# A block with dilated attention and a gated delta rule on one core: exponentials of the second half of heads taken as one wide block, and probabilities turned by a diagonal matrix of reciprocals

## The chip, the cores and the metric

The kernel runs on one core of one Trainium2 chip. The metric is the device time of one execution in microseconds (us), given as the median of several runs. Engines are named as in the profile: PE is TensorE's matmul, PEld its weight load, DVE is VectorE, ACT is ScalarE, POOL is GpSimd, SP is SyncE, which issues the DMAs.

## The reference

The reference computes one transformer block on 1024 tokens of width 1024 in float32. The input is normalised and modulated, and one projection makes queries, keys and values for 8 attention heads and for 8 delta-rule heads of width 64. Then:

```
# attention, per head and per branch (window, dilation)
s = where(valid, q k^T / 8 + bias, -1e30);  e = exp(s - max)
o_i, lse_i = e v / sum(e), max + log(sum(e));  o = sum_i softmax(lse)_i o_i

# gated delta rule, per head, in chunks of 64 tokens
q, k, v = silu(causal_conv(...));  q, k scaled by 1/|q|, 1/|k|
decay[c,e] = exp(gcum[c] - gcum[e])        for c >= e
a = tril(beta k k^T * decay, -1);  (u, w) = (I + a)^-1 (beta v, beta k exp(gcum))
qk = tril(q k^T * decay)
state scan over chunks:  v' = u - w S;  o = (q exp(g)) S + qk v';  S = S exp(g_last) + (k exp(g_last - g))^T v'
```

Both outputs are projected by `w_out`, added to the input, and a gated feed-forward layer with a last normalisation follows.

## The kernel before, in words

**The stages.** The three attention branches are merged into one masked softmax with a summed bias. Large products split each float32 operand into a high and a low part of type fp32r and add three products (lines 582-616, 1589-1599). After the input normalisation the delta rule is done in two halves of four heads, `delta(0)` and `delta(1)` (line 1207), then attention for 4 pairs of heads and 8 query blocks (`attend`, line 1369), the output projection, the feed-forward layer with a seven-product scheme on halves, and the end.

**What sets the order of the work.** A scheduler puts each engine's instructions in an order of its own: what is written first goes first, and what is written later is taken forward where the earlier work isn't ready and its buffers are free. `urgent()` gives a block precedence. `tc.issue_after(x)` puts instructions behind `x` on the same engine and adds no other wait. A generator, `others()` (line 1148), hands out the projections that the latency-bound stages are filled with: z of half 0, then k, q and v of the second half of the delta heads, then z of half 1 (`z1`), then the attention projections. Small products stand in `with turn(name)` (line 576): the table `FILL` (line 43) says how many us of that generator are written ahead of a name, and the small products go behind the last product so written. `"trq3_0False": 2.56` stands ahead of the last transposes of `delta_early`, `"kk1_0_0_q": 6.4` and `"trv2_0": 12.8` ahead of products of `delta(1)`. The results of the generator go through two PSUM banks (`gbank`, line 147, tag `g`, `bufs` 2).

**The z projection.** `proj_t` (line 602) makes 128x256 outputs, eight per half, of 24 products each. `z_evac` (line 630) empties the bank with a Silu on ACT (line 634), and POOL scales the result by a gain.

**The second half of the delta heads.** `delta_early` (line 1195), written at the end of `delta(0)`, loads four tiles of projections (k, k, q, q), does the causal convolution (`conv`, line 550: a scaled copy on ACT, three multiply-adds on DVE, a Silu on ACT), turns the tile on PE for the squared norms (`delta_turn`, line 729) and stores it in DRAM (`cv`). The tiles `cv0` to `cv3` have the tag `dt` of pool `pr`, which has two buffers. `delta(1)` loads them again, and `delta_prep` (line 754) makes the decay factors. `delta_rows` (line 704) broadcasts the rows of the summed gates `G` from DRAM to four 128x1024 tiles (one for each head, tag `lu`, five buffers), and POOL masks them (line 716). For half 1, ACT takes the logarithm of the squared norms (line 765) and, by an exponential of -0.5 of it, the factors `rk` (line 767). Then ACT makes 32 exponentials of 128x128 (line 771), whose per-partition bias carries both the factor of the key and minus the gate sum. The products of keys and queries (line 800) are multiplied by these tiles (line 806). Two more broadcast tiles, `eb`, also with the tag `dt`, are loaded and exponentiated (lines 830-839) and scale the queries. `delta_v` (line 845) convolves the values, `delta_inverse` (line 867) inverts the triangular matrices, and `delta_scan` (line 973) runs over the eight chunks.

**Attention.** `att_score` (line 1295) makes one head's 128 rows of scores (two fp32r products for each bank), a DVE instruction adds the bias and takes the row minimum (line 1312), ACT exponentiates and sums the rows (line 1317), DVE takes the reciprocal of the sum (line 1318), and POOL multiplies the row block `X` by it in place (line 1319). `att_turn` (line 1324) turns every 128x128 block of `X` on PE against the identity (line 1332), and ACT or DVE copies the banks out (lines 1335, 1337). `att_value` (line 1340) multiplies by the values (line 1353).

## Time and profile before

| what | us |
|---|---|
| runs | 1403.87, 1399.05, 1405.15; median 1403.87 |
| the profiled execution's own time | 1399.13 |
| its span, first to last instruction | 1397.3 |
| second half of delta heads: `delta_early` to the values' transposes | about 277 to 345 in the span |
| attention, with projections as fill | about 478 to 662 |
| output projection left over, second part, norm | about 662 to 750 |
| feed-forward layer | about 750 to 1397 |

Times in rows of the profile are us from the first instruction of the span, unless marked ns. A group row ends with its busy time and the mean ns of one instruction, and behind a second bar stand the idle time ahead of it and what ended most of that. A row of the view by source line or tile gives the shortest, median and longest duration in ns and the first and last start. A row of the timeline gives start, duration, engine and line, with a count where neighbours are merged. TensorE's fp32 products appear as more than one record each, so counts of records and of calls in the code can differ. "128*128" is the part of the array that is used.

### The profile page before, as it was taken

The page shows a single profiled execution, that of the slowest core. Times are in us where ns is not written, and L with a number is a line of the kernel's source. Part 1 is how long each engine was busy: PE and PEld are TensorE (multiplying, and loading weights), DVE is VectorE, ACT ScalarE, POOL GpSimd, SP SyncE. Part 2 cuts the span into 40 slices and gives each one's busy share as a digit, 9 for nine tenths or more (in the row PEclk, how much of TensorE's full clock was granted, in tenths as well). Part 3 has the DMA queues.
Part 4 walks back from the last instruction along what each step waited for, and adds up shares of the span by engine and source line. Part 5 has one row for each costly group of instructions (what it writes and reads, how often), then busy time and mean ns, then how long its engine had stood idle before and what let it go on. Part 6 is the DMA issues. An engine that isn't in the chain of part 4 may idle for free.

```text
span 1397.3 us, 24428 instructions
## 1 busy us (share of the span) xinstructions
PE 1343.9 (96%) x8984; PEld 1109.9 (79%) x8984; DVE 878.8 (63%) x1677; ACT 661.4 (47%) x1287; POOL 283.6 (20%) x267
## 2 busy tenths in 40 slices
PE   8999999998999899999999999999999999999998
PEld 5778877888888777778877788888888888888876
DVE  3688484656836433676238977667575776474497
ACT  4498424356234254775157633333333333444455
POOL 2346412443213244443262000000000000000000
PEclk9999999999999999999999999999999999999999
DMA  8666575486352455541584355455453665766585
GB/s 310 230 190 168 160 212 168 131 259 184 106 152 69 124 141 177 152 110 58 187 269 151 113 159 181 158 163 173 133 200 108 213 210 191 255 222 192 195 262 197
DMA packets 169872, 245.68 MB, mean 176 GB/s; under 512 B 32566, under 2 KB 73831, under 8 KB 169752
## 3 DMA queue, kind: packets, MB, share of 16 engines
q1 hardware_dynamic: 169752, 244.12, 55.3%
q8 instruction: 71, 1.16, 0.3%
q14 instruction: 49, 0.40, 0.1%
HBM read 181.30 MB, written 67.48 MB: 178 GB/s over the span
## 4 chain that ended last, share of the span: by engine, by line
PE 53%; DVE 5%; DMA 3%; issue 2%; ACT 2%; POOL 1%; SPq 0%; DVEq 0%; ACTq 0%; POOLq 0%
PE wua L1596 9%; PE wga L1596 8%; PE X L1796 6%; PE wuc L1596 4%; PE wgc L1596 4%; PE wo L590 4%; PE g_a L590 3%; PE wgb L1596 2%; PE Z L1796 2%; PE Y L1796 2%; PE wub L1596 2%; PE y L1353 2%; PE tr L1332 2%; PE S L1308 1%; PE S L1309 1%
## 5 line engine op out<-in xcount | busy, mean ns | idle before, releaser
L1586 DVE TENSOR_TENSOR wl_db<-wr_db,wh_db 128x512 fp32r<-128x512 f32 x77 | 52.9, 690 | 66.4 <-ACT wh_db L1585 66.4
L1585 ACT CAST wh_db<-wr_db 128x512 fp32r<-128x512 f32 x77 | 47.4, 620 | 85.7 <-PE X L1796 39.4
L1312 DVE CUSTOM_DVE_ANT_0 X<-S,ng 128x512 f32<-128x512 f32 (+3 forms) x64 | 36.9, 587 | 57.2 <-PE S L1309 43.7
L1319 POOL TENSOR_SCALAR X<-X,sc 128x128 f32<-128x128 f32 (+7 forms) x64 | 48.7, 764 | 76.3 <-DVE sc L1318 72.3
L1796 PE MATMUL X<-wl_db,wh_da 128*128 128x512 f32 x160 | 62.4, 390 | 0.3 <-DVE wl_db L1586 0.3
L1796 PE MATMUL X<-wh_db,wl_da 128*128 128x512 f32 x160 | 62.3, 389 | 0.0
L1796 PE MATMUL X<-wh_db,wh_da 128*128 128x512 f32 x160 | 62.3, 389 | 0.0
L1317 ACT ACTIVATE X<-X,sc 128x128 f32<-128x128 f32 (+7 forms) x64 | 49.5, 775 | 24.3 <-DVE sc L1312 22.7
L1586 DVE TENSOR_TENSOR wl_da<-wr_da,wh_da 128x512 fp32r<-128x512 f32 x77 | 52.8, 685 | 3.7 <-ACT wh_da L1585 3.6
L1585 ACT CAST wh_da<-wr_da 128x512 fp32r<-128x512 f32 x77 | 47.5, 616 | 15.0 <-DMA wr_da<-ao_d 8.1
L590 PE MATMUL g_a<-hh,wh_a 128*128 128x512 f32 x128 | 52.7, 412 | 0.0
L590 PE MATMUL wo<-yl,wh_wo 128*128 128x512 f32 x128 | 50.6, 396 | 1.9 <-DVE yl L1416 1.9
L590 PE MATMUL g_a<-hh,wl_a 128*128 128x512 f32 x128 | 51.7, 404 | 0.0
L590 PE MATMUL wo<-yh,wh_wo 128*128 128x512 f32 x128 | 51.6, 406 | 0.0
L590 PE MATMUL g_a<-hl,wh_a 128*128 128x512 f32 x128 | 51.4, 401 | 0.0
L590 PE MATMUL wo<-yh,wl_wo 128*128 128x512 f32 x128 | 51.1, 399 | 0.0
L1332 PE MATMUL tr<-ident,X 128*128 128x128 f32 x288 | 45.8, 278 | 5.1 <-POOL X L1319 2.4
L1585 ACT CAST wh_wg_s<-wg_s 128x512 fp32r<-128x512 f32 x33 | 20.5, 623 | 57.6 <-PE wuc L1596 24.4
L1332 PEld LDWEIGHTS tr<-ident,X 128*128 128x128 f32 x288 | 32.8, 140 | 17.0 <-POOL X L1319 6.2
L231 POOL TENSOR_TENSOR wl_wo<-wr_wo,wh_wo 128x512 fp32r<-128x512 f32 x24 | 32.2, 1344 | 59.1 <-ACT wh_wo L230 54.9
L1585 ACT CAST wh_wu_s<-wu_s 128x512 fp32r<-128x512 f32 x33 | 20.4, 621 | 43.8 <-PE wga L1596 17.2
L1585 ACT CAST wh_wg<-wr_wg 128x512 fp32r<-128x512 f32 x31 | 19.2, 622 | 46.3 <-PE wua L1596 18.9
(553 smaller groups left out, 4370.0 us busy)
## 6 DMA issues: line engine op xcount, KB each, us to landing
wm<-in_wada SPq DMA_DIRECT2D x44, 512.0 KB, 6.3
wr_da<-ao_d SPq DMA_DIRECT2D x77, 256.0 KB, 3.1
wr_wu<-in_wu SPq DMA_DIRECT2D x50, 256.0 KB, 2.7
wr_wg<-in_wg SPq DMA_DIRECT2D x48, 256.0 KB, 2.9
ao_d<-a SPq DMA_DIRECT2D x44, 256.0 KB, 2.4
wr_wd<-in_wdn SPq DMA_DIRECT2D x44, 256.0 KB, 3.0
wr_db<-wt_d SPq DMA_DIRECT2D x44, 256.0 KB, 2.7
ao_d<-as SPq DMA_DIRECT2D x33, 256.0 KB, 2.0
```

The costliest lines, as they stand in the source:

```text
L231: (eng or nc.gpsimd).tensor_tensor(out=lo[:, :n], in0=raw[:, :n], in1=hi[:, :n].bitcast(F32), op=ALU.subtract)
L590: last[0] = nc.tensor.matmul(ps, a[:, w0], b[k0 + k4][:, cs], start=(i == 0), stop=(i == n - 1))
L1308: nc.tensor.matmul(ps[:, 0 : c1 - c0], QS[:, qs], KS[:, c0:c1], start=True, stop=False)
L1312: nc.vector.tensor_tensor_reduce(out=X[:, c0:c1], in0=ps[:, 0 : c1 - c0], in1=ng[:, u + c0 : u + c1], scale=1.0, scalar=(3e38 if m is None ...
L1317: nc.scalar.activation(X[:, 0:nk], X[:, 0:nk], AF.Exp, scale=-1.0, bias=m, accum_out=sc[:, 2:3])
L1319: nc.gpsimd.tensor_scalar(out=X[:, 0:nk], in0=X[:, 0:nk], scalar1=sc[:, 3:4], scalar2=0.0, op0=ALU.mult, op1=ALU.add)
L1332: nc.tensor.transpose(ps[:, (kb - c0) * P : (kb - c0 + 1) * P], X[:, kb * P : kb * P + P], ident)
L1353: ins = nc.tensor.matmul(yps[64 * e : 64 * e + 64, (q % 4) * P : (q % 4 + 1) * P], va[:, kb, 64 * e : 64 * e + 64], ets[q % 2][e][:, kb, : ...
L1585: nc.scalar.copy(hi, src)
L1586: (eng or nc.vector).tensor_tensor(out=lo, in0=src, in1=hi.bitcast(F32), op=ALU.subtract)
L1596: nc.tensor.matmul(ps, a[:, w0], b, start=(first and k == 0 and n_ == 0), stop=(k == 3 and n_ == 2), skip_group_check=True,)
L1796: nc.tensor.matmul(bank[b], a[:, ts_], w, start=(first and n_ == 0), stop=(last and n_ == 2), skip_group_check=True,)
```

## The change

Three things are done.

1. In attention, POOL's multiplication of `X` is gone. DVE makes a diagonal matrix `dg` (the identity times the reciprocals, 128x128), and each block of `X` is turned by an ordinary fp32 product with `dg` in place of the transpose against the identity.
2. For the second half of the delta heads, the rows of `G` and the two `eb` tiles are loaded in `delta_early` behind the last convolution, DVE subtracts the gate sums from the four row tiles, and ACT exponentiates the six tiles whole, one behind the other, after the last convolution's Silu. The Silus written after that (those of the values' convolution and of `z_evac`) are put behind the last of these exponentials on ACT. The factor of the keys is multiplied in by DVE in `delta_prep`.
3. For that half the inverse root of the squared norms is a power on POOL, in place of a logarithm and an exponential on ACT.

The store of a convolved tile to `cv` is written ahead of its transposes. The tile `mhalf` is wider by 12 columns, and a spare tile is narrower by as many.

```diff
@@ conv, z_evac
+    behind = [None]
...
-        nc.scalar.activation(dst, dst, AF.Silu)
+        with tc.issue_after(behind[0].ins) if behind[0] else ExitStack():
+            return nc.scalar.activation(dst, dst, AF.Silu)
...
-            with urgent():
+            with urgent(), tc.issue_after(behind[0].ins) if behind[0] else ExitStack():
                 taken[0] = nc.scalar.activation(zt, ps[:, 0:256], AF.Silu)
@@ delta_rows, behind the mask
+            if g:
+                nc.vector.tensor_tensor(
+                    out=dt_, in0=dt_, op=ALU.subtract,
+                    in1=bc(Gc[:, 32 * g : 32 * g + 32].rearrange("p (n h) -> p n h", n=8)[:, :, hl_], P),
+                )
             dts.append(dt_)
         return dts
+
+    def delta_exps(last):
+
+        lts = delta_rows(1)
+        ebs = [delta_eb(1, q) for q in range(2)]
+        for t in (*lts, *ebs):
+            with tc.issue_after(last.ins):
+                last = nc.scalar.activation(t, t, AF.Exp)
+        behind[0] = last
+        return lts, ebs
+
+    def delta_eb(g, q):
+
+        eb = pr.tile([P, 8, P], F32, name=f"eb{2 * g + q}", tag="dt", bufs=2)
+        for e in range(2):
+            nc.sync.dma_start(
+                eb[64 * e : 64 * e + 64],
...
+            )
+        return eb
@@ delta_turn
+        if norms and kind == "k" and g:
+            v = norms["rk"][:, :, 2 * q : 2 * q + 2]
+            nc.gpsimd.tensor_scalar(out=v, in0=v, scalar1=EPS, scalar2=None, op0=ALU.add)
+            nc.gpsimd.tensor_tensor(
+                out=v, in0=v, in1=mhalf.rearrange("p (n e) -> p n e", e=2), op=ALU.pow,
+            )
@@ delta_prep
-        if g == 1:
-            nc.scalar.activation(lr, rk, AF.Ln, bias=eps1)
-        nc.vector.tensor_scalar(out=lr, in0=lr, scalar1=-0.5, scalar2=None, op0=ALU.mult)
-        nc.scalar.activation(rk, lr, AF.Exp)
-        nc.vector.tensor_tensor(out=lr, in0=lr, in1=g3(Gc), op=ALU.subtract)
-        for h in range(4):
-            for n in range(8):
-                nc.scalar.activation(lts[h][:, n], lts[h][:, n], AF.Exp, bias=lr[:, n, h : h + 1])
+        if g == 0:
...
+        else:
+            for h in range(4):
+                nc.vector.tensor_tensor(out=lts[h], in0=lts[h], in1=bc(rk[:, :, h], P), op=ALU.mult)
...
+            if ebs:
+                eb = ebs[q]
+            else:
+                eb = delta_eb(g, q)
+                nc.scalar.activation(eb, eb, AF.Exp)
@@ delta_early
-            conv((4 if kind == "k" else 0) + 2 + q, fetch(j, f"{kind}{2 + q}"), t)
+            last = conv((4 if kind == "k" else 0) + 2 + q, fetch(j, f"{kind}{2 + q}"), t)
+            nc.sync.dma_start(_.cv[j], t)
+            if j == 3:
+                made = delta_exps(last)
             delta_turn(1, kind, q, t, norms=norms[1])
-            nc.sync.dma_start(_.cv[j], t)
+        return made
@@ att_score, att_turn
-        nc.gpsimd.tensor_scalar(
-            out=X[:, 0:nk], in0=X[:, 0:nk], scalar1=sc[:, 3:4], scalar2=0.0, op0=ALU.mult, op1=ALU.add
-        )
-        return X
+        dg = pa.tile([P, P], F32, name=f"dg{h}_{qb}", tag="dg", bufs=4)
+        nc.vector.tensor_scalar(out=dg, in0=ident, scalar1=sc[:, 3:4], scalar2=None, op0=ALU.mult)
+        return X, dg
...
-                    nc.tensor.transpose(ps[:, (kb - c0) * P : (kb - c0 + 1) * P], X[:, kb * P : kb * P + P], ident)
+                    nc.tensor.matmul(
+                        ps[:, (kb - c0) * P : (kb - c0 + 1) * P], X[:, kb * P : kb * P + P], dg, start=True, stop=True,
+                    )
```

In the branch `g == 0` of `delta_prep`, the half 0 keeps the five statements that are removed above, without the logarithm, which it takes elsewhere.

More of the change, by code (lines that the diff above doesn't have):

```diff
@@ L1230, in delta @@
         delta_scan(g, st)
-        if g == 0:
-            delta_early()
-    delta(0)
-    delta(1)
+        return None if g else delta_early()
+    delta(1, delta(0))
     until(lambda: EARLY - 1 in done)
```

34 lines of the change are left out of this document (17 added, 17 removed).

## The prediction

> **What bounds the kernel now.** I read the page first (engines' shares), then the table by stretches, then the waits of PE in the two stages that the change touches.
>
> ```profile
> PE 1343.9 (96%) x8984; PEld 1109.9 (79%) x8984; DVE 878.8 (63%) x1677; ACT 661.4 (47%) x1287; POOL 283.6 (20%) x267
> ...
> 276.00:320.00 44.00, 40.43 (x395) 36.61 (x395) 22.88 (x44) 26.25 (x48) 19.94 (x20) 1.00 0.82 254
> 320.00:345.00 25.00, 20.94 (x214) 19.35 (x213) 17.39 (x22) 15.92 (x39) 9.29 (x7) 0.91 0.60 150
> 478.00:662.00 184.00, 174.66 (x1280) 140.09 (x1280) 96.94 (x314) 113.71 (x255) 78.16 (x82) 0.99 0.46 135
> 665.00:695.00 30.00, 30.00 (x140) 24.64 (x137) 8.21 (x11) 3.70 (x6) 6.43 (x5) 1.00 0.59 194
> ```
>
> The first row is the page's: PE is busy for 96% of the span. In the other rows the columns are stretch, length, busy us (instructions) of PE, PEld, DVE, ACT, POOL, then PE's granted clock. Attention (478 to 662) keeps PE busy for 174.7 of 184 us, and right behind it PE works without a gap on projections left over (665 to 695). So work added to PE in attention lengthens the kernel, except for what fits into 9.3 us of idle time. In the delta stage PE idles 3.6 us before 320 and 4.1 us after it, at a clock of 0.91. The waits of PE, from 478 to 662 and (last three rows) from 276 to 346:
>
> ```profile
> PE tr L1332 <- POOL X L1319: 2.4, 3, 1.0
> PE S L1308 <- DVE sc L1312: 2.0, 5, 1.1
> PE wo L590 <- DVE yl L1416: 1.9, 1, 1.9
> PE tr L1332 <- DVE et L1335: 1.9, 3, 0.9
> ```
>
> ```profile
> PE trv L857 <- ACT vd L557: 3.8, 1, 3.8
> PE yt L1065 <- DVE o L1055: 1.7, 3, 1.2
> PE kk_q L800 <- DMA qd<-cv_d: 0.9, 1, 0.9
> ```
>
> The POOL step that the change removes holds PE for 2.4 us in all. The exponentials that it widens hold PE only through the values' Silu behind them, 3.8 us.
>
> **Attention: what the product costs.** First the transposes of now and an ordinary fp32 product of the same shape (128x128 by 128x128) by source line, then two pieces of the timeline (start, length, records).
>
> ```profile
> L1332 PE MATMUL tr<-ident,X x288: 270/273/331, 487.8 to 660.8; 128*128 128x128 f32 x144
> ...
> L985 PE MATMUL st<-S,kd 128*128 128x128 f32 x56 | 11.8, 293 | 2.2 <-DVE S L1020 2.1
> ...
> 627.34 0.60 PE L1332 MATMUL tr<-ident,X 128*128 128x128 f32 x4
> ...
> 268.90 0.38 PE L985 MATMUL st<-S,kd 128*128 128x128 f32 x2
> ```
>
> The code calls the transpose 288 times (8 heads, 1 to 8 blocks for each of 8 query blocks), and there are 288 records: one each. Line 985 is called 28 times (7 chunks, 2 pairs, 2 halves) and has 56 records: two each. Records start (0.60 - 0.273) / 3 = 0.109 us apart in a row of transposes, and (0.38 - 0.273) = 0.107 us apart within one product. So a transpose holds PE for 0.109 us and a product for about twice that, and the change adds 288 x 0.109 = **31.4 us** to PE.
>
> The Trainium skill speaks against this edit in "Perfetto Trace Analysis", Transposes: a logical transpose should be a transpose and not a standard matmul. In "TensorE: Matmul & The Clock Gate", Terms, it calls the transpose mode 4x faster for FP32. By that factor the added work would be 288 x 3 x 0.109 = 94 us, an estimate; the records here show a factor of two, and I go by them.
>
> What is saved and added beside PE:
>
> ```profile
> L1319 POOL TENSOR_SCALAR X<-X,sc 128x128 f32<-128x128 f32 (+7 forms) x64 | 48.7, 764 | 76.3 <-DVE sc L1318 72.3
> ...
> L298 DVE TENSOR_TENSOR wbg<-wba,G 128x128 f32<-128x128 f32 x1 | 0.3, 293 | 0.0
> L1499 DVE TENSOR_TENSOR dg<-ident,r 128x512 f32<-128x512 f32 x2 | 1.4, 693 | 0.1
> ```
>
> POOL's 64 steps of 0.76 us go, and 64 diagonals come to DVE. The trace has no such instruction on one 128x128 tile with a per-partition scalar; the nearest is the 128x128 product of line 298 at 0.29 us, the other end is a quarter of the 128x512 diagonal of line 1499, 0.17. I take 0.29: 18.8 us on a DVE that is busy 97 of the stage's 184 us, hidden behind PE's own work; if that cover were gone, it would cost at most those 18.8, but POOL's 48.7 us lie at the same place in the chain and held PE for only 2.4. The chain to the transpose becomes 0.47 us shorter for each block of rows. With PE slower by a tenth in this stage, the other engines run ahead of it, so I take back the waits on POOL, on the scores and on the copies out: 2.4 + 2.0 + 1.9 = 6.3 us. Attention: 31.4 - 6.3 = **+25 us**. Bounds: all 9.3 us of PE's idle time absorbed, +22; nothing absorbed and the two DVE waits (3.9 us) doubled, +35.
>
> **The delta stage: what is saved on ACT.**
>
> ```profile
> L771 ACT ACTIVATE dt<-dt,lr 128x128 f32<-128x128 f32 x32 | 9.7, 397 | 0.0
> L557 ACT ACT_TABLE_LOAD x2 | 2.6, 1283 | 4.4 <-DVE vd L553 4.4
> L839 ACT ACTIVATE eb<-eb 128x1024 f32<-128x1024 f32 x2 | 2.1, 1054 | 0.4 <-issue 0.4
> ...
> L875 DVE TENSOR_TENSOR nt<-nt,bpr 128x1024 f32<-128x1024 f32 x2 | 2.4, 1221 | 14.7 <-POOL wl_qd L231 14.7
> L1053 POOL TENSOR_TENSOR of<-of,mhalf 128x4 f32<-128x4 f32 x16 | 16.3, 1016 | 20.3 <-DVE of L1050 20.2
> ```
>
> The 32 small exponentials (9.7 us busy) become four of 1.05, or 4.2 us. The logarithm and the small exponential go, and with them most of the changes between Silu's and the exponential's tables, of 1.28 us each. DVE gets eight 128x1024 operations by a broadcast factor, like line 875's 1.22 us: 9.8 us, four ahead of the exponentials and four ahead of the products with the keys. POOL's power is shown for 4 columns at 1.02 us; for 16 it is between 1.02 and 4.1, twice, and the key norms are done about 15 us before they are used, so I cost it at nothing; uncovered it would delay the products by up to 8 us. None of this is on PE's path except in front of the values' transposes: with the exponentials gone from behind 315 us, the values' convolution no longer has to follow them, and the wait of 3.8 us goes.
>
> **The delta stage: the wait that is added.** All Silus that are written after the wide exponentials go behind the last of them on ACT, whatever engine order the scheduler would choose. Which ones are these? Adding up the `FILL` entries in the order of the program, the generator stands in the last v projection when `delta_exps` is reached: the first product of `z1` is written by `"trq3_0False"`, just behind it. So all eight z evacuations of this half wait. In the trace they run early, as a filling of the scan and of the convolutions:
>
> ```profile
> L634 ACT ACTIVATE zt<-g_z x8: 361/381/384, 278.6 to 313.9; 128x256 f32<-128x256 f32 x8
> ...
> 282.45 0.28 PE L613 MATMUL g_z<-wh_z,hl 128*128 128x256 f32 x1
> 282.57 0.28 PE L613 MATMUL g_z<-wl_z,hh 128*128 128x256 f32 x1
> ```
>
> One z tile is 24 records 0.12 us apart, 2.9 us. Two fit into the two `g` banks, and the others can't start until the first bank is emptied. Six tiles, **17.3 us** of PE's work, are thus pushed behind the exponentials. When do these end?
>
> ```profile
> 302.53 2.59 DVE L553 SCALAR_TENSOR_TENSOR cv<-xp_q,cw,cv 128x1022 f32<-128x1022 f32 x2
> ...
> 306.54 1.06 ACT L557 ACTIVATE cv<-cv 128x1024 f32<-128x1024 f32 x1
> ...
> L1202 SPq DMA_DIRECT2D cv_d<-cv x2: 320/329/338, 303.1 to 307.6; - x2
> ...
> DMA to landing us min/median/max: 5.0/5.0/5.0
> ...
> L832 SPq DMA_DIRECT2D eb<-G_d x4: 627/634/685, 322.0 to 324.1; - x4
> ...
> DMA to landing us min/median/max: 5.1/5.1/5.1
> ```
>
> The last convolution ends on DVE at 305.1; its Silu no longer waits for table loads, so it ends at 306.2. The second `eb` tile needs a `dt` buffer, and both are in use: it gets that of `cv3`, which is free when its store has landed, 5.0 us later. Its load takes 5.1, the exponential 1.05, the table load back to Silu 1.28 and the first evacuation 0.38: about **319 us** in place of 278.6. The load sits in SP's queue meanwhile with what is issued after it, the loads of the stored tiles among them; those need the same store and lose little. From about 290, where the third z tile would run, until 319 PE has only transposes to do, and the products of keys and queries stand behind the fill of `"kk1_0_0_q"`, which needs the third z tile. So beside the 17.3 us about 3 us of work that PE did before 319 are late too (projections of va and the first of these products, whose place is seen in the wait at line 800): 20 us. After 319 PE has fill without end, and gets back the 3.8 us of the values' wait and some 1.5 of other short ones (its wait on DVE at line 1055 is 1.7). The delta stage: 20.3 - 5.3 = **+15 us**. Low bound: if the exponentials end so early that no z tile is late, only the 3.8 us stay, -4. High bound: if DVE's four subtractions stand ahead of the last convolution step, 4 x 1.22 = 4.9 us later, and 2 us of short waits come back less than I assume, +22.
>
> The clock: after the wait of 3.8 us the table's row 320 to 345 shows 0.91, which is 0.09 x 25 = 2.3 us lost. The new wait is longer, so I expect the same loss at about 320 and count no gain. The Trainium skill says in "TensorE: Matmul & The Clock Gate", HAM oscillation, that idle gaps over some 3.4 us bring the clock down; the row agrees, and by that page a gap of 20 us costs again one such stretch and the sum doesn't change.
>
> **The sum.** 25 + 15 = +40 us. Against the profiled execution's own time of 1399.13 that is 1439; this execution lies 4.7 us under the median of 1403.87, and from the median it is **1444 us**. Bounds: 22 - 4 = +18, or 1422; 35 + 22 = +57, or 1461. I widen the low side to 1417 for the rivals.
>
> **The rivals.**
> - *The z tiles are not held up*: the scheduler, or earlier loads, ends the exponentials near 300. For it: `G` rows are ready early, and only one `dt` buffer is critical. Against: the store and load of 10 us behind the last Silu. Then the delta stage gives -4 and the kernel takes 1403.9 + 25 - 4 = 1425. Chance 0.20.
> - *Faster: the chain of the row block, not PE, sets attention's pace.* Then the product's second record costs nothing, and each of 64 row blocks is 0.47 us shorter: -30, with the delta stage +15: 1389. It decides if PE's free time in the stage is over 31 us. For it: POOL is named ahead of the transposes. Against: PE idles 9.3 us, 2.4 of them behind POOL. Chance 0.05; the same with the chain half as long a limit, an end within 0.5%, has 0.02.
> - *The product takes four passes*, as the page's factor says: four records of 0.109 for each. Then 94 - 6 + 15 = +103, 1507. Against: two records for each call of line 985. Chance 0.03.
> - *The stall spreads*: ACT's order behind the exponentials also holds copies that PE needs, for another 15 us or more: over 1461. Chance 0.04.
>
> **How the numbers follow.** The forecast has 0.66. The range from 1417 to 1461 takes in the first rival and the forecast. A difference of 0.5%, 7 us, is about what can be told from no change here. Slower: 0.66 + 0.20 + 0.03 + 0.04 = 0.93; within: 0.02; faster: 0.05.
>
> **What would show it.** The products in place of the transposes: 576 records, 0.11 us apart, and PE's busy time up by some 31 us in attention, with its stretch about 25 us longer. All eight evacuations of the second z half behind the last of six exponentials of 1.05 us, at about 319 us; PE idle for some 20 us between 290 and 319, named as waiting for ACT; no wait of 3.8 us at the values' transposes. Wrong would be the forecast if the product had 288 records, if PE's idle time in attention fell by more than 10 us, or if z evacuations stood ahead of the exponentials.

## The result, and the profile after

| | before | after |
|---|---|---|
| median of runs, us | 1403.90 (1399.05 to 1405.15) | 1467.42 (1467.01 to 1473.01) |
| profiled execution / its span, us | 1399.13 / 1397.3 | 1467.23 / 1465.5 |

After against before is 1.0468 (95% interval 1.0433 to 1.0504), 63.5 us slower; the forecast was 40 us, 1444. The page after: engine totals, TensorE's clock in 40 slices of 36.6 us, and the group of the turns.

```profile
PE 1394.0 (95%) x9272; PEld 1158.4 (79%) x9272; DVE 903.7 (62%) x1747; ACT 654.3 (45%) x1253; POOL 241.5 (16%) x207
...
PEclk9998999967999999999999999999999999999999
...
L1366 PE MATMUL tr<-dg,X 128*128 128x128 f32 x576 | 77.2, 279 | 4.7 <-DVE et L1371 2.8
```

The 576 records are there. The clock row has a dip that the forecast does not account for: 6 and 7 in the ninth and tenth slice, 293 to 366 us, the second half of the delta heads. That place in the table by windows, columns as in the prediction, before and then after:

```profile
290.00:350.00 60.00, 52.93 (x510) 48.64 (x509) 38.30 (x49) 39.99 (x78) 23.42 (x19) 0.94 0.75 216
```

```profile
290.00:350.00 60.00, 37.83 (x361) 28.12 (x361) 30.35 (x46) 24.23 (x36) 19.71 (x14) 0.63 0.64 212
```

From 290 to 350 TensorE has 361 records instead of 510, at a clock of 0.63, and idles 22.2 us for 7.1. Where the time went is read from fixed points in the work (view by tile, first and last start): the transposes of the delta outputs (`yt`, the last ends the delta stage), the first turn of a stored tile, and the products with the values (the last ends attention). Before, then after:

```profile
L1065 PE MATMUL yt<-ident,o x32: 270/273/421, 255.9 to 475.5; 128*128 128x128 f32 x32
...
L738 PE MATMUL trk_0False<-ident,cv x8: 272/272/273, 292.3 to 294.0; 128*128 128x128 f32 x8
...
L1353 PE MATMUL y<-et,va x576: 272/273/476, 493.1 to 665.2; 128*64 128x128 f32 x192
```

```profile
L1099 PE MATMUL yt<-ident,o x32: 270/273/476, 264.7 to 509.8; 128*128 128x128 f32 x32
...
L769 PE MATMUL trk_0False<-ident,cv x8: 272/376/421, 313.8 to 315.9; 128*128 128x128 f32 x8
...
L1389 PE MATMUL y<-et,va x576: 272/273/323, 529.0 to 730.1; 128*64 128x128 f32 x192
```

The stored tiles are turned 21.5 us later (292.3 to 313.8), the delta stage ends 34.3 us later (475.5 to 509.8), attention 64.9 us later (665.2 to 730.1). So attention cost 30.6 us, near the forecast's 25, and the delta stage 34.3 where 15 was forecast. (These are differences of the two profiled executions, which lie 68.1 us apart, as that of before is 4.8 under its median.)

The same two parts as stretches of equal work, from 100 us to the last `yt`, and from there to the end of the output projection's last product `wo`. Before, then after:

```profile
100.00:475.50 375.50, 354.45 (x3483) 310.15 (x3484) 230.96 (x484) 166.49 (x366) 134.66 (x120) 0.98 0.53 154
475.50:751.30 275.80, 262.40 (x1734) 211.32 (x1735) 136.23 (x364) 152.84 (x323) 117.32 (x111) 0.99 0.51 155
```

```profile
100.00:509.80 409.80, 371.55 (x3488) 322.48 (x3487) 238.70 (x491) 157.86 (x334) 142.36 (x124) 0.92 0.47 142
509.80:821.90 312.10, 297.04 (x2022) 248.88 (x2022) 154.92 (x428) 155.52 (x323) 69.08 (x47) 0.99 0.45 137
```

In the first part nearly the same records (3483 and 3488) take 17.1 us more of busy time, at a clock of 0.92 for 0.98, and TensorE idles 17.2 us more. In the second part, which holds attention, there are 288 records more, 34.6 us more of busy time at the same clock, and almost the same idle time (15.1 us for 13.4). So attention is no different in kind from before: it has more work on a TensorE that was busy already.

Of the delta stage's loss a large part exists *before* the exponentials run: the convolution chain starts late. The timeline of SP's queue says by what, before and then after:

```profile
283.84 1.90 SPq L1120 DMA_DIRECT2D wm<-in_wada  x2
285.84 0.42 SPq L1045 DMA_DIRECT2D zl<-zg_d  x1
```

```profile
292.42 14.44 SPq L1154 DMA_DIRECT2D wm<-in_wada  x10
306.92 0.46 SPq L1079 DMA_DIRECT2D zl<-zg_d  x1
...
312.62 0.42 DVE L1089 TENSOR_TENSOR o<-o,zl 128x256 f32<-128x256 f32 x1 [5.31 <-DMA zl<-zg_d]
```

`wm` are weights of the modulation, whose products are one more filling of TensorE. Before, two of these loads stand ahead of the load of a gate tile `zl`, which the end of the first half's scan needs. After, ten do, and SP takes 14.4 us over them. The gate tile is loaded 21 us later, and VectorE waits for it (last row). TensorE's timeline of the same time, after:

```profile
295.44 1.08 PE L211 MATMUL mods<-wm,cc 128*32 128x128 f32 x32
298.36 0.99 PE L211 MATMUL mods<-wm,cc 128*32 128x128 f32 x16 [1.83 <-DMA wm<-in_wada]
...
312.29 1.08 PE L211 MATMUL mods<-wm,cc 128*32 128x128 f32 x16 [0.54 <-DMA wm<-in_wada]
313.30 0.69 PE L1099 MATMUL yt<-ident,o 128*128 128x128 f32 x2
313.79 1.06 PE L769 MATMUL trk_0False<-ident,cv 128*128 128x128 f32 x4
```

From 295 to 313 there is nothing but modulation, load by load; then the scan's output that needed the gate tile is turned, and behind it the first stored tile.

ScalarE behind the last convolution, after:

```profile
329.77 1.06 ACT L560 ACTIVATE cv<-cv 128x1024 f32<-128x1024 f32 x1 [2.04 <-DVE cv L555]
330.85 1.28 ACT L737 ACT_TABLE_LOAD   x1
332.14 3.90 ACT L737 ACTIVATE dt<-dt 128x1024 f32<-128x1024 f32 x4
...
341.80 1.06 ACT L737 ACTIVATE eb<-eb 128x1024 f32<-128x1024 f32 x1
342.88 1.28 ACT L637 ACT_TABLE_LOAD   x1
344.18 0.66 ACT L637 ACTIVATE zt<-g_z 128x256 f32<-128x256 f32 x2
```

The first evacuation of a z tile starts at 344.2, the last of the eight at 374.0; the forecast had the first end at about 319. The path from the last Silu to the start of the first has nearly the forecast's length: 344.18 - 330.83 = 13.4 us, against 12.4 (319 - 306.2, less the evacuation's own 0.38). The start of the path is wrong, by 24.6 us.

For the 22.2 us that TensorE idles from 290 to 350, the view by waits does not name the held evacuations. It names the loads of `wm` (5.9 us), the convolutions' Silus (5.7) and `nbp` (4.8), a factor that VectorE makes from the result of GpSimd's powers. The second power ends at 328.08, and `nbp` follows at 329.66. In e11 below, which has no power, the wait on `nbp` is 2.5 us. No run prices the power by itself.

A second, smaller delay is seen on VectorE at the first scan, before and then after:

```profile
248.53 0.94 DVE L1018 COPY S<-st 64x64 f32<-64x64 f32 x4 [4.33 <-PE st L1009]
```

```profile
253.48 2.28 DVE L724 TENSOR_TENSOR dt<-dt,Gc 128x1024 f32<-128x1024 f32 x1 [6.21 <-POOL dt L719]
255.77 0.95 DVE L1052 COPY S<-st 64x64 f32<-64x64 f32 x4
```

The first of the new subtractions stands ahead of the scan's first copy of the state. It waits 6.2 us for GpSimd's mask and takes 2.3, and the copy, 248.5 before, runs at 255.8.

### The profile page after: what moved, and what is told of

Same layout as the page of the kernel before. It is cut to its first block, busy times and chain, and to the rows that moved or that the text cites. A ratio compares the mean times of both kernels' runs of the same rounds, so it can differ in the third digit from the quotient of the medians.

```text
span 1465.5 us, 24871 instructions
## 1 busy us (share of the span) xinstructions
PE 1394.0 (95%) x9272; PEld 1158.4 (79%) x9272; DVE 903.7 (62%) x1747; ACT 654.3 (45%) x1253; POOL 241.5 (16%) x207
## 5 line engine op out<-in xcount | busy, mean ns | idle before, releaser
L1366 PE MATMUL tr<-dg,X 128*128 128x128 f32 x576 | 77.2, 279 | 4.7 <-DVE et L1371 2.8
L1366 PEld LDWEIGHTS tr<-dg,X 128*128 128x128 f32 x576 | 71.3, 191 | 12.7 <-ACT et L1373 5.1
L231 POOL TENSOR_TENSOR wl_wo<-wr_wo,wh_wo 128x512 fp32r<-128x512 f32 x24 | 32.1, 1339 | 129.7 <-ACT wh_wo L230 104.9
L1373 ACT COPY et<-tr 128x512 f32<-128x512 f32 (+3 forms) x64 | 31.3, 500 | 20.9 <-PE tr L1366 20.7
```

Source lines behind the costliest of these rows:

```text
L231: (eng or nc.gpsimd).tensor_tensor(out=lo[:, :n], in0=raw[:, :n], in1=hi[:, :n].bitcast(F32), op=ALU.subtract)
L1366: nc.tensor.matmul(ps[:, (kb - c0) * P : (kb - c0 + 1) * P], X[:, kb * P : kb * P + P], dg, start=True, stop=True,)
L1373: nc.scalar.copy(eo, ps[:, 0 : (c1 - c0) * P])
```

## The experiments

Medians, each against the runs of the kernel before on the same chip; the ratio has its 95% interval.

| run | what it is | us | over before | ratio |
|---|---|---|---|---|
| e1 | attention part alone | 1434.20 | +32.1 | 1.0225 (1.0208 to 1.0241) |
| e2 | delta part alone | 1434.16 | +32.1 | 1.0225 (1.0210 to 1.0241) |
| e3 | after, modulation held back | 1460.76 | +58.7 | 1.0428 (1.0403 to 1.0452) |
| e4 | after, z evacuations free | 1441.91 | +39.8 | 1.0279 (1.0261 to 1.0297) |
| e5 | after, subtractions behind the scan | 1460.98 | +58.2 | 1.0422 (1.0394 to 1.0451) |
| e6 | e1 with one record, one score tile | 1427.68 | +24.9 | 1.0197 (1.0156 to 1.0239) |
| e7 | before, scaling on VectorE | 1401.12 | -1.7 | 0.9982 (0.9962 to 1.0002) |
| e8 | delta part without its holds | 1407.76 | +5.0 | 1.0042 (1.0024 to 1.0061) |
| e9 | e1 with one record, two score tiles | 1427.07 | +24.9 | 1.0182 (1.0157 to 1.0208) |
| e10 | e9, other buffers | 1427.07 | +24.9 | 1.0181 (1.0158 to 1.0203) |
| e11 | before, z evacuations held | 1425.84 | +23.7 | 1.0171 (1.0136 to 1.0206) |
| e12 | e9 with two records | 1428.85 | +26.7 | 1.0200 (1.0166 to 1.0234) |
| e13 | before, order written out | 1402.89 | +1.6 | 1.0005 (0.9987 to 1.0024) |
| e14 | one record in e13's order | 1427.26 | +26.0 | 1.0169 (1.0131 to 1.0206) |
| e15 | two records in e13's order | 1429.92 | +28.6 | 1.0195 (1.0151 to 1.0239) |
| e16 | before, unscaled, idle diagonals | 1394.81 | -6.5 | 0.9957 (0.9936 to 0.9978) |
| e17 | e14, fillers in order too | 1418.88 | +14.0 | 1.0109 (1.0066 to 1.0152) |
| e18 | e14, identity for the diagonal | 1436.76 | +31.9 | 1.0232 (1.0184 to 1.0280) |

**e1 and e2: the two halves of the change.** e1 is the kernel before with the edits of `att_score` and `att_turn` alone, e2 has all the others.

> The kernel before with the diagonal product in attention alone; the delta stage is the old one. Theory (PE's second record is paid in full): the transposes' place shows 576 records 0.11 us apart, PE's busy time in attention rises by about 31 us, and the kernel takes 1403.9 + 31 to 33, 1434 to 1437 us. Rival 1 (the forecast's term: waits on POOL and on the copies are absorbed): 1427 to 1430. Rival 2 (the two parts of the change disturb each other, and attention alone costs less than the stage's shift of 30.5 us in the changed kernel): under 1427.

> The changed kernel with attention as before: POOL multiplies the rows and PE transposes against the identity. Theory: the delta stage alone costs what its end is late in the changed kernel, 34.3 us less 3.1 that stand ahead of the change, so 1403.9 + 31 = 1435 us, within 4 us. Rival (the forecast's size): 1403.9 + 15 = 1419 us. If the sum of this and of the attention-alone kernel's shift is not 63.5 us within 6, the parts disturb each other.

Each is 32.1 us over the kernel before; together that is 64.2, and the whole change cost 63.5. The parts add up, so each can be studied alone. In the stretch from the last `yt` to the last `wo`, e1 has 34.4 us more of busy time than the kernel before (296.8 for 262.4) and 14.0 us idle for 13.4: the second records filled none of the idle time.

### The delta stage

**e4: nothing held but the values' Silu.**

```diff
@@ after, z_evac
-            with urgent(), tc.issue_after(behind[0].ins) if behind[0] else ExitStack():
+            with urgent():
```

> The changed kernel with the order behind the wide exponentials taken from the z evacuations alone; the Silu of the values' convolution keeps it. Theory (the held evacuations cause both the idle PE and the modulation loads that run ahead): the z evacuations run from about 287 on as before, PE's idle time between 285 and 345 falls from over 20 us to under 8, and the kernel takes 1467.4 - 25 = 1442 us (1437 to 1448); some 4 us more table loads on ACT come back. Rival 1 (the wide exponentials and DVE's new work set the time themselves): over 1458. Rival 2 (the delta part is a gain without the hold, by the 3.8 us at the values' transposes): under 1437.

23.7 us come back of the change's 63.5. In its profile two modulation loads stand ahead of the gate tile again, and the turns of stored tiles start at 300.5, not 313.8.

**e11: the hold by itself, in the kernel before.**

```diff
@@ before, z_evac; behind[0] is None up to the last stored tile, then that tile's Silu
-            with urgent():
+            with urgent(), tc.issue_after(behind[0].ins) if behind[0] else ExitStack():
```

> The kernel before with one thing of the change: the z evacuations of the second half of heads stand in ScalarE's order behind the Silu of the last stored tile. No wide exponential, no power on GpSimd, the old attention. Theory: this hold alone lets the modulation products and their loads run ahead, the load of z stands behind them in SP's queue, and the convolution chain starts late; the first z evacuation comes at 320 to 330 us and the time is 15 to 25 us over the kernel before, 1417 to 1428 us. Rival: the wide exponentials and the power are needed for the delay; then 1402 to 1408 us.

The theory's time: +23.7 us without a single wide exponential. By tile and on SP's queue:

```profile
L739 PE MATMUL trk_0False<-ident,cv x8: 402/421/473, 311.1 to 313.6; 128*128 128x128 f32 x8
...
L635 ACT ACTIVATE zt<-g_z x8: 365/384/385, 327.5 to 363.7; 128x256 f32<-128x256 f32 x8
```

```profile
288.75 15.18 SPq L1121 DMA_DIRECT2D wm<-in_wada  x10
303.98 0.46 SPq L1046 DMA_DIRECT2D zl<-zg_d  x1
```

The ten loads ahead of the gate tile are there, the stored tiles are turned at 311.1 (before 292.3), at a clock of 0.53 from 311 to 314 (421 ns for 272), and the z evacuations start at 327.5 though the order that was added puts them behind one Silu only. With e4 this makes the hold the cause of about 24 of the stage's 32 us, whatever it waits for.

**e3: the modulation kept from running ahead.**

```diff
@@ after, mod_rows
-                rows4(ps, cc[:, k : k + 32], w, 4, k == KT - 1, k == 0)
+                with tc.issue_after(last[0].ins) if last[0] else ExitStack():
+                    rows4(ps, cc[:, k : k + 32], w, 4, k == KT - 1, k == 0)
```

> The changed kernel with one order added: each modulation product goes behind the last projection product that was written ahead of it, on PE. Nothing else is changed. In the changed kernel ten modulation loads (292.4 to 306.9 us) stand ahead of one small load (zl) in SP's queue, and the last turn of the scan, the transposes and the convolutions come 21 us late. Theory (that queue is what makes the wait longer than forecast): two modulation loads stand ahead of that load, the first transposes of the stored tiles start at about 300 in place of 313.8, the last wide exponential ends at about 330 in place of 342.9, and the kernel takes 1467.4 - 12 = 1455 us (1449 to 1459). Rival (the loads only fill a queue that is idle anyway; the chain of store, load and exponential sets the time): the transposes start within 3 us of 313.8 and the time is 1464 to 1470.

Between theory and rival. The queue is put right: two loads ahead of the gate tile, the turns of stored tiles at 298.0 instead of 313.8, 15.8 us earlier. But the time falls by 4.8 only, and the intervals of e3 and of the whole change overlap. With no z tile and no modulation, TensorE has little to fill the chain with: the window from 290 to 350 shows 38.7 us busy at a clock of 0.69, and the last modulation product starts at 401.3, in the changed kernel at 313.0. So the overtaken queue explains where the delay sits. What it costs by itself e3 can't say, since e3 takes a filler away with it.

**e5: the subtractions behind the scan.**

```diff
@@ after, delta_rows; scanned[0] is the last state update of the first half
+                with tc.issue_after(scanned[0].ins):
                     nc.vector.tensor_tensor(out=dt_, in0=dt_, op=ALU.subtract, ...
```

> The changed kernel with one order added: DVE's four subtractions of the gate sums go behind the last state update of the first half's scan. In the changed kernel the first of them stands ahead of the first state copy on DVE and waits there for its mask (252 to 255.8 us); PE waits 3.8 us and then has half its clock for 6.8 us. Theory: the scan of the first half ends 5.5 us earlier, and with it all that follows: 1467.4 - 5.5 = 1462 us (1459 to 1464). Rival (the time is lost again in the queue of modulation loads, which PE and SP reach anyway): 1466 to 1469.

The theory's time: 5.3 us less than after. The slowest of its runs (1462.2) is below the fastest of the changed kernel (1467.0), but the intervals of the two ratios, each against its own runs of the kernel before, overlap.

**e8: the delta part without these delays.** The old attention, z evacuations free, the subtractions behind the scan, and the values' scaled copy on ScalarE behind the last stored tile's Silu, since in e4 it stood in front of that tile and waited for its load (8.3 us of TensorE's waits).

> The delta part of the change without its holds, attention as before: z evacuations are free of the order behind the exponentials, DVE's subtractions go behind the scan of the first half, and the scaled copy of the values' convolution goes behind the Silu of the last stored tile on ACT (with the z evacuations free alone, that copy stood ahead of the Silu and waited 8.3 us for its load). Theory: with the z evacuations free the delta stage ended 11.8 us late; 5.5 of these were the subtraction and about 7 the Silu behind the copy, so the stage ends as before and the kernel takes 1402 us (1396 to 1407). Rival 1 (the wide exponentials, POOL's power and DVE's eight operations cost by themselves): over 1410. Rival 2 (they gain the 3.8 us at the values' transposes): under 1396.

+5.0 us, just above the expected interval and far from 32: most of the price was in what the edits held up, and what is left of them saves nothing either. Which of the wide exponentials, GpSimd's powers and VectorE's eight new operations costs the 5.0 us was not tried.

### Attention

**e7: GpSimd's hop priced.** The kernel before with the scaling of `X` on VectorE and the transposes kept.

> The kernel before with the multiplication of the row blocks by their reciprocals on DVE in place of POOL; PE transposes as before. Theory (POOL's step holds PE for 2.4 us in all, and DVE has room): 1402 - 2, 1398 to 1403 us, no difference that can be told. Rival (the chain through POOL sets attention's pace more than its named waits say): under 1395.

No difference: the hop that the change removes is worth nothing measurable.

**e16: the diagonals priced.** The scaling is left out; VectorE makes the diagonals, and nothing uses them.

> The kernel before with GpSimd's scaling left out (the probabilities stay unscaled) and the 64 diagonals made on VectorE as in the change, used by nothing; the turns stay transposes. It prices the diagonals on VectorE by themselves. Theory (VectorE has room, 104 of 210 us busy in the stage): 1397 to 1406 us, no difference. Rival (the 64 x 0.306 = 20 us on VectorE delay evacuations and scores): 1412 to 1427 us.

6.5 us *faster* than before, and below the expected range. Leaving out the scaling and making 64 diagonals on VectorE is together a gain, so the diagonals cost less than the scaling did. What they cost by themselves isn't shown, as no run leaves out the scaling alone. No version that computes the reference beat the kernel before measurably.

**e6, e9, e10, e12: one record for two.** Exponentials into their own fp32r tile `E`, the diagonal in fp32r, so that a product is one record. e9:

```diff
@@ e1, att_score
+        E = pa.tile([P, T], F32R, name=f"E{h}_{qb}", tag="E", bufs=4)
-        nc.scalar.activation(X[:, 0:nk], X[:, 0:nk], AF.Exp, ...
+        nc.scalar.activation(E[:, 0:nk], X[:, 0:nk], AF.Exp, ...
-        dg = pa.tile([P, P], F32, ...
+        dg = pa.tile([P, P], F32R, ...
```

> The kernel before with the diagonal product in attention in one pass: the exponentials go to a tile of type fp32r and the diagonal is fp32r too, so the probabilities are rounded to that type. The score tile has one buffer and the tile of exponentials four, in place of five score tiles. Theory (PE's records are the cost): 288 records, about 0.06 us apart as the fp32r score products of 128 columns are, so PE has 288 x 0.05 = 14 us less than with transposes, and some 2 us of waits on POOL go: 1402 - 16 = 1386 us (1381 to 1392). Rival 1 (the weight load or the single-record spacing of 0.109 us is the limit, not the passes): 1398 to 1403. Rival 2 (the chain by way of DVE's diagonal is the cost): over 1410.

> The kernel before with the diagonal product in one pass (probabilities and diagonal rounded to fp32r) and two score tiles beside four tiles of exponentials. Theory: the time of e6 above the kernel before came from its single score tile (the scores' subtraction waited for the exponential); with two the attention's PE work, 288 x (0.109 - 0.057) = 15 us less than with the transposes, shows, and the time is 1385 to 1395 us. Rival: what holds e6 is not the score tile but the longer chain from the exponential through the reciprocal, the diagonal and the evacuation; then it stays at 1410 to 1430.

> As e9, but three tiles of exponentials and six turned tiles instead of four and five. Theory (the score tile was the limit in e6): within 5 us of e9, 1385 to 1395 us. Rival (buffers of the exponentials or of the turned tiles are the limit): differs from e9 by more than 5 us, in the direction that names which of the two is short.

> The kernel of e9 with the product left in fp32, two records of 0.109 us a block: same buffers, same order. Theory (PE's records are the cost of the attention part): 288 x (0.217 - 0.057) = 46 us above e9 if PE stays the bound in both, so 1431 to 1440 us, e1's time. Rival (the buffers hold both): within 15 us of e9.

All four lie within 2 us of each other, 25 to 27 us over before. The theory of the score tile falls with e9 and e10. Nor does a product without the second record give the price back: e9 has 288 records less than e12 and takes 1.8 us less, which is within the spread of their runs. One expectation was also wrong in size: most one-record products stand 0.11 us apart, as transposes do (rows below), not 0.057. The stretch from the last `yt` to the last `wo`, e12 first, then e9:

```profile
476.20:783.00 306.80, 293.26 (x2022) 246.33 (x2022) 154.19 (x428) 155.28 (x323) 68.81 (x47) 1.00 0.47 139
```

```profile
475.80:776.40 300.60, 274.24 (x1734) 221.66 (x1734) 153.20 (x428) 153.54 (x323) 68.34 (x47) 0.97 0.47 142
```

Against the kernel before (262.4 us busy, 13.4 idle), e12 has 30.9 us more of busy time at full clock and no more idle time (13.5). So its loss is the second records, like that of e1 and of the change. e9 has the 1734 records of before and loses in another way: 13.0 us more idle time, and 11.8 us more of busy time at a lower clock. What the records gave back, waits and clock took. From 480 to 690 the clock is 0.95 in e9, 0.99 before and 1.00 in e12, and no wait that is named there is longer than 2.5 us. The Trainium skill describes such a case in "TensorE: Matmul & The Clock Gate", A second HAM failure mode: psum-queue depth-cycling, where short idle times between groups that cycle through banks bring the clock down; the 0.95 of e9 agrees.

The one-record versions also have other tiles than before: one or two score tiles and three or four tiles of exponentials, in place of five of `X`. Three sizes gave the same time (e6, e9, e10), but no run makes transposes out of such tiles.

**e13, e14, e15: the order fixed.** TensorE's order of scores, turns and values is written out as the kernel before has it, and `att_score` and `att_turn` are called piece by piece along that list, each piece behind the one before (`pinned()` is `tc.issue_after` of the last product of the piece ahead):

```diff
@@ attend
+ORDER = "S0_0_0 S1_0_0 S0_1_0 S1_1_0 tr0_0_0 S0_2_0 S1_2_0 tr1_0_0 ..."
-            with turn(f"et{h}_{qb}_{c0}"):
+            with turn(f"et{h}_{qb}_{c0}"), pinned():
```

> The kernel before with TensorE's order of the attention (scores, turns, values) written out, name by name, as the scheduler had made it for the kernel before. It is the control for the next two, which have the same list. Expected: 1400 to 1412 us; what it stands above the kernel before is the price of writing the order out (the filling products can't move as freely).

> The diagonal product in one record (fp32r, the tiles of e9), in the written order of e13. In e9 one record a block took TensorE's time of a transpose (0.11 us apart) and the time was still 25 us over the kernel before, with the scheduler's own order: turns in runs of 16 with no scores between them. Theory (that order is e9's cost): within 6 us of e13. Rival (the diagonal, the separate tiles or the evacuations cost it): 15 to 25 us above e13.

> The diagonal product in fp32 (two records of 0.109 us a block) in the written order of e13, score tiles as before. Theory (two causes, each enough by itself: the second records and the order): 288 x 0.109 = 31 us less what waits are absorbed, so 22 to 31 us above e13 and about as much above e14. Rival (only the order counts): within 8 us of e13.

The control equals the kernel before, and the product is 24 us over it with one record and 27 with two. So the order of scores, turns and values is not the cause. Over the work from the last `yt` to the last `wo`, e15 has 28.3 us more of busy time than e13 (293.2 for 264.9, both at a clock of 0.99) and no more idle time: with two records the loss is again the records. e14 has as many records as e13, 11.9 us more idle time, and 17.2 us more of busy time at a clock of 0.93. What the list leaves free is the place of the filling products (`g_a`, `wo`). One stretch of TensorE's timeline, e13 and then e14:

```profile
538.02 0.93 PE L1366 MATMUL tr<-ident,X 128*128 128x128 f32 x7
538.70 0.47 PE L610 MATMUL g_a<-hh,wh_a 128*128 128x512 f32 x1
...
542.76 1.09 PE L1366 MATMUL tr<-ident,X 128*128 128x128 f32 x8 [0.85 <-POOL X L1351]
543.61 0.47 PE L610 MATMUL g_a<-hh,wh_a 128*128 128x512 f32 x1
```

```profile
534.35 0.89 PE L1366 MATMUL tr<-dg,E 128*128 128x128 f32 x7
...
536.91 0.66 PE L1366 MATMUL tr<-dg,E 128*128 128x128 f32 x4 [0.46 <-ACT et L1373]
539.12 0.62 PE L1366 MATMUL tr<-dg,E 128*128 128x128 f32 x3 [1.54 <-DVE et L1371]
...
540.85 2.91 PE L1366 MATMUL tr<-dg,E 128*128 128x128 f32 x12 [0.25 <-DVE et L1371]
```

Seven records in 0.89 us are 0.10 us apart, like the transposes in the first row. In e13 eight turns fill the two banks and fillers follow while the banks are copied out. In e14 twelve turns stand together: a bank has to be emptied before the last four can run. TensorE waits 0.46, 1.54 and 0.25 us for the copies `et`, and the twelve, of 0.42 us each, stand (2.91 - 0.42) / 11 = 0.23 us apart, twice as far as the seven, after the gap of 1.5 us.

**e18: the product without a diagonal.** e14's order, GpSimd scales as before (into the fp32r tile), and the turn is a product with a constant identity.

> In the written order of e13 and e14: GpSimd scales the probabilities as before (into an fp32r tile), and the turn is a product with a constant identity in fp32r. No diagonal is made, and nothing waits for VectorE beyond the reciprocal. If the product (one record a block, 0.11 us apart) and the place of the fillers that comes with it are the cost, 1420 to 1430 us as e14; if the diagonal on VectorE, with evacuations queued behind it, is the cost, 1400 to 1408 us as e13.

+31.9, above both expected ranges. There is no diagonal, and the loss stays: it needs neither the diagonal nor VectorE's part in making it. That the form of the turn, a product in place of a transpose, costs all of it is not shown. e18 also has e14's two score tiles, which GpSimd reads as well, and TensorE waits 7.7 us on the scores and 3.4 on GpSimd's scaling, in e13 4.4 and 1.3.

**e17: the fillers in their places too**, in threes.

```diff
@@ attend
+            if name[0] == "G":
+                due += int(name[1:])
+                while 3 * given + 1 < due and next(fill[0], None):
+                    given += 1
```

> The kernel of e14 (diagonal product in one fp32r record) with the filling products put in the written order too, in threes, where the kernel before has them: in e14 the scheduler had left them out from between the turns, so that turns stood in runs of 12 and 16 with two banks to turn into. Theory (the runs of turns without fillers make TensorE wait for the evacuations and the clock fall): 1400 to 1410 us, at most 4 us of waits on the evacuations and no half clock beyond 7 us in the stage. Rival (the product or its diagonal costs it in any order): 1420 to 1430 us, as e9, e10 and e14.

+14.0, between theory and rival: about half of e14's loss goes with the fillers back between the turns. From the last `yt` to the last `wo`, e14 and then e17:

```profile
473.00:783.00 310.00, 282.15 (x1734) 229.30 (x1734) 155.00 (x428) 155.17 (x323) 68.40 (x47) 0.93 0.46 138
```

```profile
474.10:770.70 296.60, 270.61 (x1734) 221.72 (x1734) 157.57 (x428) 154.55 (x323) 70.01 (x47) 0.97 0.47 144
```

The same records take 11.5 us less of busy time, at a higher clock; the idle time falls by 1.9 us only (27.9 to 26.0). The theory named waits and clock. What came back is slow records and hardly any waiting: TensorE's waits on the copies out of the turn banks are even longer, 17.3 us in e17 for 13.4 in e14 (476 to 710). Most are for ScalarE's copies, e13 and then e17:

```profile
PE tr L1366 <- ACT et L1371: 1.5, 1, 1.5
```

```profile
PE tr L1374 <- ACT et L1381: 7.9, 7, 2.9
PE y L1396 <- ACT et L1381: 5.3, 5, 3.3
```

I had written out TensorE's order, not ScalarE's and VectorE's. Whether their orders, made for the product too, are the other half was not tried and stays open. No run writes out the fillers with the transposes kept, so a part of the 14.0 us can also be the price of the list. Open as well is why the scheduler treats the product differently; that it counts a product longer than a transpose fits, and is only argued.

## Why the prediction was wrong

**What bounds the kernel.** Right: TensorE was busy in attention, nothing could be added to it free of charge, and the change is slower. The size was not: 63.5 us for 40, outside the range.

**Attention, +25 forecast, +31 measured** (30.6 in the profile, 32.1 in e1). The records (576, two for a call, 0.11 us apart) and their price were as forecast: 31.4 us, for 34.4 us more of busy time in e1. The term that failed is the 6.3 us of waits that the forecast took back: the idle time did not fall (14.0 us in e1 for 13.4). After, TensorE still waits 2.8 and 1.9 us on the copies out and 2.3 on the scores:

```profile
PE tr L1366 <- DVE et L1371: 2.8, 5, 0.7
PE S L1343 <- DVE sc L1347: 2.3, 2, 1.3
...
PE tr L1366 <- ACT et L1373: 1.9, 3, 0.8
```

The measured loss lies inside the bounds of +22 to +35, and the mechanism holds for the change as it was made: two records, paid in full. It does not hold for the product as such. e9 and e14 have one record, a transpose's price on TensorE, and lose 25 and 26 us all the same, to waits on the copies out and to a lower clock; with two records (e12 and e15) it is 2 to 3 us more. With fillers put back between the turns 12 of e14's 26 us come back (e17); the cause of the rest is open. So a sum of records alone would have forecast no loss for the one-record product.

**The diagonals, POOL's hop.** Right: 0.287 us median for the diagonal (forecast 0.29), no wait of TensorE's on it is named in the changed kernel's attention, and the hop is worth nothing measurable (e7).

**The delta stage, +15 forecast, +32 (e2) measured: the step that failed.** That all eight z evacuations are held was right, and so was the length of the path from the last Silu to the first of them (13.4 us for 12.4). What failed is the step before: the last Silu was put at 306.2, where the convolutions stood in the trace of before. The forecast said that from 290 to 319 TensorE "has only transposes to do", and it asked of SP's queue only what stands behind the load of `eb`, which would "lose little". With the z tiles out of TensorE's filling, the modulation was taken forward in their place, its ten loads stood ahead of the gate tile's, and the chain that the hold itself waits for began about 20 us later. e11 shows this loop with the hold alone, e4 shows 23.7 us coming back without it, and e3 suggests that it isn't the queue alone: with the queue put right the chain is early and the time hardly better. How much of the 23.7 us is the late chain and how much the missing filling, no run separates. The 5.3 us of waits that the forecast gave back don't show either: the wait at the values' transposes is gone, and the new ones are longer. The hold (23.7, e11), the subtractions (5.3, e5) and what e8 keeps (5.0) add up to 34.0 us, near the 32.1 of e2.

**DVE's subtractions and POOL's power.** The forecast kept the subtractions as a high bound of 4.9 us at the last convolution. They cost 5.3 us (e5), at another place, the first scan, behind a wait for GpSimd's mask that the working had not named. The power was put at nothing, up to 8 us if uncovered. It does not look covered: TensorE waited 4.8 us for what is made from it, in e11 without it 2.5, and its own price is open.

**The clock.** The forecast counted no further loss, beyond some 2.3 us as before. From 290 to 350 the clock was 0.63 against 0.94, and the turns of the stored tiles, which the chain waits for, took 376 ns median for 272. The Trainium skill's rule in "TensorE: Matmul & The Clock Gate", HAM oscillation (idle gaps bring the clock down), agrees with that row. "The sum doesn't change" was my error: over the same work of the delta part TensorE's busy time grew by 17.1 us at the lower clock. How much of that lies on the path that ends last isn't shown.

**The rivals.** None came as described. The nearest, "the stall spreads" beyond 1461 us with a chance of 0.04, had the time, but laid it to copies held on ScalarE; what is seen is the overtaken queue, the missing fillers and the lower clock. That the z tiles are not held (0.20), four passes (0.03) and a faster chain (0.05) are excluded by the rows above.

## What to carry to other kernels

When an order puts work behind something late, ask what takes the place of the work that is held, which queues that substitute runs through, and whether the late thing itself stands behind them: here the hold alone delayed what it waited for, 24 us with nothing else changed (e11). A filler can be worth more than its own time where it hides a chain: the forecast had 17.3 us of filling moved, and moving it cost 23.7. And taking a record off a busy TensorE is not yet a gain of time: idle time and clock can take it back (one record or two, 25 to 29 us lost). Count busy time, idle time and clock over the same work, before and after; the three tell apart what the time alone does not.

## What the runs showed of the hardware

GpSimd's power takes 2.93 us for 16 columns, against 1.02 for 4 in the kernel before; after:

```profile
320.43 2.93 POOL L786 TENSOR_TENSOR rk<-rk,mhalf 128x16 f32<-128x16 f32 x1
```

VectorE's diagonal, 0.29 us by itself, took 2.07 us where GpSimd was at work, and ended 0.08 us after it (604.07 and 603.99; timeline of e14):

```profile
601.61 2.38 POOL L1304 TENSOR_TENSOR KL<-raw,KS 128x1024 fp32r<-128x1024 f32 x1
...
602.00 2.07 DVE L1353 TENSOR_SCALAR dg<-ident,sc 128x128 fp32r<-128x128 f32 x1
```

The Trainium skill says in "GPSIMD Engine Reference", 1. Specifications, that GpSimd shares its SBUF interfaces with VectorE, with contention where a VectorE instruction runs in a 2-port perf mode or has two SBUF inputs. These rows agree with the sharing; which of the two cases this is, they don't show.

A product of 128x128 by 128x128 in fp32r, one record, is no denser than a transpose of the same block: both stand 0.10 to 0.11 us apart (seven in 0.89 us in e14, in 0.93 us in e13). The weight loads ahead of them differ, 0.192 us in the median for the product and 0.140 for the transpose; whether that bears on the loss was not tried.
